# Down projection of a hybrid decoder layer: each pass opens with a plain pair of k tiles, the last pass takes its seventh sevenfold pair earlier, and GpSimd's additions go to VectorE

## The chip, the cores and the metric

One core of a Trainium2 chip runs the whole layer as one program. The metric is device time in microseconds (us), from the first to the last instruction and what lies around them, as the median of the runs shown. The engines are TensorE (PE; its weight loads are PEld), VectorE (DVE), ScalarE (ACT), GpSimd (POOL) and SyncE (SP), each with a queue of its own that is worked through in order. DMA transfers are issued from a queue (SP's for the weights, ScalarE's for the rest) and run beside the engines.

## What is computed

A decoder layer over 256 tokens of width 2048. Two token mixers and their merge come first; this change is in the last stage, the second matrix of the MLP:

```python
h = rmsnorm(x, norm_mlp_pre[l])
u = jnp.square(jax.nn.relu(h @ w_mlp_up[l]))          # 256 x 8192
x = x + rmsnorm(u @ w_mlp_down[l], norm_mlp_post[l])   # 8192 x 2048
```

All values are float32 and the result must agree with float32 arithmetic.

## The kernel before, in words

**Two parts for one number.** TensorE multiplies float32r here, which keeps fewer bits than float32. So every operand is split in two parts, hi (a rounded copy, ScalarE, L94) and lo (what is left, VectorE, L95), and a product is three matmuls: hi by hi, hi by lo, lo by hi (`product`, L1036). Weights arrive raw by DMA and are split on the fly by the class `Stream`: four raw half chunks (`wraw`, 512 KB each), six `whi` and six `wlo`. A chunk is one pair of k tiles by 1024 columns, in two halves.

**The MLP in two halves.** The hidden width 8192 is taken in two halves f = 0, 1 of 4096. For each, the up projection makes the 16 pairs of k tiles of u (`a_pair`, whose last step L261 adds two PSUM banks and so frees them; `evacuate` squares and splits). Then `down` runs twice, n = 0 and 1, over 1024 columns of the result each: four passes, here called (f, n). The passes with f = 0 leave their sum in DRAM (`acc_away`); those with f = 1 add it, and the last pass, (1, 1), also normalises and stores.

**A pass.** A pass goes over 16 pairs p of k tiles. A plain pair is 2 halves x 4 banks x 3 matmuls = 24 products of 128x512. The pairs in `SEVEN` = 0, 2, ..., 12 are done by a fast 2x2 scheme with seven products instead of eight: 7 x 3 = 21 matmuls, for which u and the weights are first combined by additions. Those of the weights are `split_sums`: VectorE makes the sums T1, T3, T4 in a tile t (L123 to L126), ScalarE rounds it to thi (L129), VectorE makes tlo (L130). These three tiles come from the pool `big` of twelve 1 MB buffers, which it shares with the activations `uT`, the accumulators and the gain. A pass has eight PSUM banks: four named s (for the products P1, P6, Q5, N7; the up projection's pairs live in the same four) and four of their own, Q3, P2, Q4 and Cs. The four quarters of the result, (token half tb, column half i), end in Q4, Cs, P2 and Q3 (`PLACE`).

**The order of a pass.** The pairs come as 0, 1, 2, ..., 15. After the seventh sevenfold pair, 12, the four s banks are combined into four tiles `ready` (L1077 to L1081), and `early` adds the accumulator to them (L1145): on VectorE, but in the last pass for tb = 1 on GpSimd. Pairs 14 and 15 are held back (`held` = 2) and done quarter by quarter, so that `finish` (L1162) can take one bank while TensorE fills the next. In the last pass the quarters come as (0, 0), (0, 1), (1, 0), (1, 1), and after each second one `finish` does the norm (L334 to L336), the residual (L1175) and the store. `between` multiplies a quarter of the accumulator by the gain g3 (L1155) behind pairs 3, 5, 7 and 9 of the last pass; g3 is loaded by ScalarE's queue (L1184), and so is x1, the residual (L1149, called from `early`).

**What sets the order of the queues.** A scheduler orders the instructions of each engine by the order in which the program gives them, with some look-ahead, and puts in the waits. `Stream.ahead` runs the splits six halves ahead of TensorE. So the order in which the weights are listed (`chunks`, and `sums`, which says which of them are sevenfold) sets what VectorE, ScalarE and the weight loads do, and when.

Of the kernel before, what the change touches and what calls it, by code (L numbers as in the profile page):

```python
# [22 lines left out]
ALU = mybir.AluOpType  # L23
# [15 lines left out]
SEVEN = (0, 2, 4, 6, 8, 10, 12)  # L39
PAIRS = 16  # L40


# [124 lines left out]
def layer(tc, x, g_pre, pos_t, pos_row, inv_freq, vecs, sinks, gains, w_kv, w_q, w_xy, w_rg, w_g, w_rp, w_ap, w_out,  # L167
# [37 lines left out]
    for f in range(2):  # L205
        chunks += [w_up[32 * f + i] for i in range(32)]
        for n in range(2):
            sums.update(len(chunks) + i for i in SEVEN)
            chunks += [w_dn[(2 * f + n) * PAIRS + i] for i in range(PAIRS)]

# [832 lines left out]

    def down(f, n, uT, held, order, finish, early, between=lambda p: None):

# [7 lines left out]
        def step(p, parts, names):  # L1053
            for name in names:
                at, n2 = name
                b = PLACE[name]
                for i, (hi, lo) in enumerate(parts):
                    t = slice(at * P, at * P + P)
                    c = quarter(n2)
                    a = uT[p][:, i]  # L1060
                    product(banks[b], (a[:, 0, t], a[:, 1, t]), (hi[:, c], lo[:, c]), b in begun,
                            p == PAIRS - 1 and i == 1)
                    begun.add(b)

        ready = {}
        for p in range(PAIRS - held):
            if p in SEVEN:
                parts = ws.seven()
                for name, (i, w) in LEFT.items():
                    product(banks[name], (uT[p][:, 0, i], uT[p][:, 1, i]), parts[w], name in begun,  # L1070
                            p == SEVEN[-1] and name in ("P1", "P6", "Q5", "N7"))
                    begun.add(name)
                if p == SEVEN[-1]:
                    for name in ((1, 0), (0, 0), (1, 1), (0, 1)):
# [6 lines left out]
                    v.tensor_tensor(ready[0, 1], ready[1, 1], banks["N7"], ALU.add)  # L1081
                    early(ready)
            else:
                for i in range(2):
                    hi, lo = ws.half()
                    for name in order:
                        at, n2 = name
# [4 lines left out]
                        begun.add(b)  # L1092
            between(p)
        parts = [[ws.half(False) for i in range(2)] for p in range(held)]
        for name in order:
            for i in range(held):
                step(PAIRS - held + i, parts[i], (name,))
            finish(name, banks[PLACE[name]], ready[name])
        ws.ahead(ws.at - 1)

    for f in range(2):
# [3 lines left out]
        for p in range(PAIRS):  # L1105
# [11 lines left out]
            if f == 1 or p >= R2_AT:  # L1117
# [7 lines left out]
                full.clear()  # L1125
        order = [(1, 1), (1, 0), (0, 0), (0, 1)]
        if f == 0:
            for n in range(2):
# [5 lines left out]

                down(f, n, uT, 2, order, finish, lambda ready: None)
            continue
# [5 lines left out]
        def early(ready):  # L1142
            for (tb, i), t in ready.items():
                c = quarter(2 * n + i)
                (nc.gpsimd if n and tb else nc.vector).tensor_tensor(t, t, acc[tb][:, c], ALU.add)  # L1145
            if n == 1:
# [3 lines left out]

        def between(p):
            if p in (3, 5, 7, 9):
                tb, q = divmod((p - 3) // 2, 2)
                c = quarter(q)
                nc.vector.tensor_tensor(acc[tb][:, c], acc[tb][:, c], g3[:, c], ALU.mult)  # L1155
# [22 lines left out]
        n = 0  # L1178
        down(f, n, uT, 2, order, finish, early)
        n = 1  # L1180
# [3 lines left out]
        nc.scalar.dma_start(g3, gains[3].partition_broadcast(P))  # L1184
        down(f, n, uT, 2, [(0, 0), (0, 1), (1, 0), (1, 1)], finish, early, between)
    ctx2.close()
# [73 lines left out]
```

## Time and profile before

| what | value |
|---|---|
| median of 3 runs | 1527.35 us (1525.62 to 1528.20) |
| the profiled execution, its own time | 1523.52 us |
| its span, first to last instruction | 1521.7 us |
| granted clock of TensorE, mean | 0.999 |
| TensorE busy | 1506.0 us (99%) |
| VectorE busy | 1105.1 us (73%) |
| ScalarE busy | 831.3 us (55%) |
| GpSimd busy | 5.5 us, 11 instructions |
| first product of the first down pass | at 1003.36 us |
| last product of the kernel | starts at 1511.89 us |

The page lists the busy time of each engine over the whole span. The views of the trace give single instructions: when each began, how long it took, and in brackets how long its engine had sat idle before it and what ended that.

### The profile page before, as it was taken

How to read it: one execution, taken by the hardware profiler on the slowest of the kernel's cores; microseconds unless marked ns; L12 is line 12 of the kernel's file. 1: busy time of each engine (PE TensorE's matmuls, PEld its weight loads, DVE VectorE, ACT ScalarE, POOL GpSimd, SP SyncE). 2: the span in 40 equal slices, each digit the busy share in tenths (PEclk: the TensorE clock that was granted, in tenths of full speed). 3: DMA queues.
4: the chain of work that ended last, by engine and by line, in shares of the span. 5: the costliest groups of instructions: out<-in, count | busy, mean ns of one | idle time of the engine just before them, and what ended most of it. 6: DMA issues, size and time to landing. Idle time of an engine off the chain costs nothing.

```text
span 1521.7 us, 20058 instructions
## 1 busy us (share of the span) xinstructions
PE 1506.0 (99%) x7600; PEld 1263.7 (83%) x7600; DVE 1105.1 (73%) x1377; ACT 831.3 (55%) x1143; POOL 5.5 (0%) x11
## 2 busy tenths in 40 slices
PE   9999999999999999999999999999999999999997
PEld 7877778788888888888888888888888888888886
DVE  6666666857759867555667866688886766788897
ACT  6545645746556757444355655555444555555553
POOL 0000000000000000000000000000000000000001
PEclk9999999999999999999999999999999999999999
DMA  6645445354655565555764755556667655566665
GB/s 252 221 153 166 138 142 168 128 188 161 215 184 189 169 219 177 197 195 191 263 225 131 274 198 189 187 182 216 213 202 237 205 187 192 188 230 200 216 221 178
DMA packets 82896, 296.20 MB, mean 195 GB/s; under 512 B 9712, under 2 KB 9968, under 8 KB 81648
## 3 DMA queue, kind: packets, MB, share of 16 engines
q1 hardware_dynamic: 79056, 284.43, 56.4%
q10 hardware_dynamic: 3744, 10.50, 1.9%
q8 instruction: 59, 0.97, 0.3%
q14 instruction: 37, 0.30, 0.1%
HBM read 288.60 MB, written 6.29 MB: 194 GB/s over the span
## 4 chain that ended last, share of the span: by engine, by line
PE 90%; DVE 4%; ACT 2%; DMA 2%; issue 2%; SPq 0%; DVEq 0%; ACTq 0%
PE ps L253 21%; PE ps L256 11%; PE dQ L1036 8%; PE s L1036 4%; PE pp L273 4%; PE pp L275 4%; PE pp L271 4%; PE dP L1036 4%; PE g L271 4%; PE g L275 4%; PE g L273 4%; PE dCs L1036 3%; PE q L271 2%; PE q L273 2%; PE q L275 2%
## 5 line engine op out<-in xcount | busy, mean ns | idle before, releaser
L95 DVE TENSOR_TENSOR wlo<-wraw,whi 128x1024 fp32r<-128x1024 f32 x523 | 634.4, 1222 | 306.2 <-ACT whi L94 304.6
L94 ACT CAST whi<-wraw 128x1024 fp32r<-128x1024 f32 x523 | 544.3, 1051 | 567.4 <-PE ps L253 139.2
L253 PE MATMUL ps<-h2T,whi 128*128 128x512 f32 x960 | 240.5, 393 | 0.0
L253 PEld LDWEIGHTS ps<-h2T,whi 128*128 128x128 f32 x960 | 172.9, 189 | 30.7
L256 PEld LDWEIGHTS ps<-h2T,wlo 128*128 128x128 f32 x960 | 131.0, 191 | 9.3
L256 PE MATMUL ps<-h2T,wlo 128*128 128x256 f32 x960 | 133.9, 283 | 0.0
L253 PE MATMUL ps<-hT,whi 128*128 128x512 f32 x512 | 130.0, 394 | 0.0
L1036 PE MATMUL dQ<-whi,uT 128*128 128x512 f32 x288 | 107.0, 389 | 0.0
L253 PEld LDWEIGHTS ps<-hT,whi 128*128 128x128 f32 x512 | 91.8, 189 | 16.8 <-issue 0.7
L271 PE MATMUL g<-whi,hT 128*128 128x512 f32 x256 | 101.7, 397 | 0.0
L273 PE MATMUL g<-wlo,hT 128*128 128x512 f32 x256 | 100.4, 392 | 0.1
L275 PE MATMUL g<-whi,hT 128*128 128x512 f32 x256 | 100.2, 391 | 0.0
L256 PEld LDWEIGHTS ps<-hT,wlo 128*128 128x128 f32 x512 | 69.8, 191 | 6.3 <-issue 1.5
L256 PE MATMUL ps<-hT,wlo 128*128 128x256 f32 x512 | 71.9, 283 | 0.0
L1036 PEld LDWEIGHTS dQ<-whi,uT 128*128 128x128 f32 x288 | 54.1, 188 | 11.2
L271 PEld LDWEIGHTS g<-whi,hT 128*128 128x128 f32 x256 | 48.1, 188 | 10.9 <-issue 1.3
L275 PEld LDWEIGHTS g<-whi,hT 128*128 128x128 f32 x256 | 48.1, 188 | 10.6 <-issue 0.7
L273 PEld LDWEIGHTS g<-wlo,hT 128*128 128x128 f32 x256 | 48.2, 188 | 9.7 <-DVE wlo L95 0.5
L1036 PE MATMUL dQ<-wlo,uT 128*128 128x512 f32 x144 | 56.1, 389 | 0.0
L130 DVE TENSOR_TENSOR tlo<-t,thi 128x1536 fp32r<-128x1536 f32 x28 | 49.2, 1757 | 6.8 <-ACT thi L129 6.8
L1036 PE MATMUL dP<-whi,uT 128*128 128x512 f32 x144 | 54.1, 389 | 0.0
L1036 PE MATMUL dCs<-whi,uT 128*128 128x512 f32 x144 | 54.1, 389 | 0.0
(280 smaller groups left out, 2477.4 us busy)
## 6 DMA issues: line engine op xcount, KB each, us to landing
wraw<-in_w_up SPq DMA_DIRECT2D x128, 512.0 KB, 4.7
wraw<-in_w_dn SPq DMA_DIRECT2D x128, 512.0 KB, 4.6
wraw<-in_w_g SPq DMA_DIRECT2D x64, 512.0 KB, 4.8
wraw<-in_w_xy SPq DMA_DIRECT2D x64, 512.0 KB, 4.6
wraw<-in_w_q SPq DMA_DIRECT2D x32, 512.0 KB, 3.7
wraw<-in_w_ap SPq DMA_DIRECT2D x32, 512.0 KB, 4.7
wraw<-in_w_rp SPq DMA_DIRECT2D x32, 512.0 KB, 4.4
wraw<-in_w_out SPq DMA_DIRECT2D x32, 512.0 KB, 5.2
```

Of the source, the lines that this page charges most:

```text
L94: self.pin(self.nc.scalar.copy(hi, src))
L95: self.pin(self.nc.vector.tensor_tensor(lo, src, hi.bitcast(F32), ALU.subtract))
L130: v.tensor_tensor(lo, t, hi.bitcast(F32), ALU.subtract)
L253: mm(both, hi[:, k * P : k * P + P], a.rearrange("p a b -> p (a b)"), start=half == 0 and k == 0, stop=False)
L256: mm(ps[:, f, 1, :], lo[:, k * P : k * P + P], a[:, 0, :], start=False, stop=half == 1 and k == 7)
L271: mm(banks[tb][n], a[:, 0, t], hi[:, n * 512 : n * 512 + 512], start=first, stop=False)
L273: mm(banks[tb][n], a[:, 0, t], lo[:, n * 512 : n * 512 + 512], start=False, stop=False)
L275: mm(banks[tb][n], a[:, 1, t], hi[:, n * 512 : n * 512 + 512], start=False, stop=last)
L1036: mm(b, a[x], w[y], start=not begun and i == 0, stop=tail and i == 2)
```

## The change

The order of the pairs within a pass is now a table: `PASS` for the first three passes and `LAST_PASS` for the last. A pass opens with the plain pair 1, and this first plain pair is done bank by bank (`step`: both halves into Q3, then P2, Q4, Cs) instead of half by half. Then come pair 0, 3, 2, 5, 4 and so on; pair 12 follows directly on pair 10. In the last pass pair 6 follows directly on pair 4, and pair 12 stands ahead of pair 11 instead of behind it. The list of weights follows the same tables, so loads and splits move with them. Plain pairs take the banks in the order `DOWN_ORDER` in every pass. `between` now counts places instead of pairs, and all additions of `early` are on VectorE.

```diff
+PASS = (1, 0, 3, 2, 5, 4, 7, 6, 9, 8, 11, 10, 12, 13, 14, 15)
+LAST_PASS = (1, 0, 3, 2, 5, 4, 6, 7, 8, 9, 10, 12, 11, 13, 14, 15)
...
         for n in range(2):
-            sums.update(len(chunks) + i for i in SEVEN)
-            chunks += [w_dn[(2 * f + n) * PAIRS + i] for i in range(PAIRS)]
+            turns = LAST_PASS if (f, n) == (1, 1) else PASS
+            sums.update(len(chunks) + i for i, p in enumerate(turns) if p in SEVEN)
+            chunks += [w_dn[(2 * f + n) * PAIRS + p] for p in turns]
...
-    def down(f, n, uT, held, order, finish, early, between=lambda p: None):
+    DOWN_ORDER = ((1, 1), (1, 0), (0, 0), (0, 1))
+
+    def down(turns, uT, held, order, finish, early, between=lambda i: None):
...
-                            p == PAIRS - 1 and i == 1)
+                            p == turns[-1] and i == 1)
...
-        for p in range(PAIRS - held):
+        final = [p for p in turns if p in SEVEN][-1]
+        for at_turn, p in enumerate(turns[:PAIRS - held]):
             if p in SEVEN:
...
-                if p == SEVEN[-1]:
+                if p == final:
...
+            elif not at_turn:
+
+                step(p, [ws.half() for i in range(2)], DOWN_ORDER)
             else:
                 for i in range(2):
                     hi, lo = ws.half()
-                    for name in order:
+                    for name in DOWN_ORDER:
...
-            between(p)
+            between(at_turn)
...
-                step(PAIRS - held + i, parts[i], (name,))
+                step(turns[PAIRS - held + i], parts[i], (name,))
...
-                (nc.gpsimd if n and tb else nc.vector).tensor_tensor(t, t, acc[tb][:, c], ALU.add)
+                nc.vector.tensor_tensor(t, t, acc[tb][:, c], ALU.add)
...
-        def between(p):
-            if p in (3, 5, 7, 9):
-                tb, q = divmod((p - 3) // 2, 2)
+        def between(i):
+            if i in (2, 4, 7, 9):
+                tb, q = divmod((2, 4, 7, 9).index(i), 2)
```

The rows of the order that follow name tiles with their numbers; `whi358` is the hi part of half chunk 358. The first pass begins with half 336, so half 336 + 2k belongs to the k-th pair of its order; the last pass begins with half 496.

TensorE's queue at the opening of the first pass, before (`s` is a bank that the up projection used, `dQ` and `dP` are banks of the pass, `seven` is u of a sevenfold pair):

```order
L1036 MATMUL s_8647<-whi_8509,seven_7318 128x512
L1036 MATMUL s_8647<-wlo_8510,seven_7318 128x512
L1036 MATMUL s_8647<-whi_8509,seven_7318 128x512
L1036 MATMUL dQ_8650<-whi_8509,seven_7318 128x512
L1036 MATMUL dQ_8650<-wlo_8510,seven_7318 128x512
L1036 MATMUL dQ_8650<-whi_8509,seven_7318 128x512
```

The same place now (`uT` is u of plain pairs):

```order
L1040 MATMUL dQ_8638<-whi_8503,uT_7069 128x512
L1040 MATMUL dQ_8638<-wlo_8504,uT_7069 128x512
L1040 MATMUL dQ_8638<-whi_8503,uT_7069 128x512
L1040 MATMUL dQ_8638<-whi_8533,uT_7069 128x512
L1040 MATMUL dQ_8638<-wlo_8534,uT_7069 128x512
L1040 MATMUL dQ_8638<-whi_8533,uT_7069 128x512
L1040 MATMUL dP_8637<-whi_8503,uT_7069 128x512
```

The sevenfold pair 0, with its s banks, has moved behind the 24 products of pair 1.

ScalarE's queue in the first pass around the cast `thi360` of pair 12, before (half 360 + 2 = 362 is pair 13 there):

```order
L129 CAST thi356_8932<-t356_8931 128x1536
L94 CAST whi360_9014<-wraw360_8947 128x1024
L94 CAST whi361_9018<-wraw361_8961 128x1024
L94 CAST whi362_9061<-wraw362_8992 128x1024
L94 CAST whi363_9065<-wraw363_8994 128x1024
L129 CAST thi360_9009<-t360_9008 128x1536
```

The same place now, where half 358 is pair 10, half 360 pair 12 and half 364 the first of the held pair 14:

```order
L132 CAST thi358_8968<-t358_8967 128x1536
L97 CAST whi361_9030<-wraw361_8953 128x1024
L97 CAST whi362_9052<-wraw362_8983 128x1024
L97 CAST whi363_9070<-wraw363_8997 128x1024
L97 CAST whi364_9097<-wraw364_9036 128x1024
L132 CAST thi360_9021<-t360_9020 128x1536
```

The cast of pair 12 comes one sevenfold pair behind that of pair 10 with no plain pair between them, and the cast of half 364 is ahead of it.

VectorE's queue at the opening of the last pass, before (L1162 finishes a bank of the pass ahead, `wlo498` is the first split of that pass's pair 1):

```order
L1162 TENSOR_TENSOR acc0_11505<-dQ4_11513,t_11993 128x512
L123 TENSOR_TENSOR t500_12125<-wraw501_12123,wraw500_12045 128x1024
L95 TENSOR_TENSOR wlo498_12116<-wraw498_12013,whi498_12115 128x1024
L1162 TENSOR_TENSOR acc0_11505<-dCs_11514,t_11995 128x512
L95 TENSOR_TENSOR wlo499_12120<-wraw499_12015,whi499_12119 128x1024
```

The same place now (`wlo498` belongs to pair 0, the second of the pass):

```order
L1172 TENSOR_TENSOR acc0_11493<-dQ4_11501,t_11993 128x512
L1172 TENSOR_TENSOR acc0_11493<-dCs_11502,t_11995 128x512
L1165 TENSOR_TENSOR acc0_11493<-acc0_11493,g3_12136 128x512
L98 TENSOR_TENSOR wlo498_12114<-wraw498_12013,whi498_12113 128x1024
L98 TENSOR_TENSOR wlo499_12118<-wraw499_12015,whi499_12117 128x1024
L98 TENSOR_TENSOR wlo500_12124<-wraw500_12033,whi500_12123 128x1024
L98 TENSOR_TENSOR wlo501_12145<-wraw501_12127,whi501_12144 128x1024
```

The first multiplication by g3 has moved from the middle of the pass to ahead of its second pair's splits, and the load of g3 on ScalarE's queue from behind the cast of half 503 to ahead of that of half 498.

## Rows read from the trace of the kernel before

**Rows 1.** The page: busy time, share of the span and instructions of each engine.

```profile
PE 1506.0 (99%) x7600; PEld 1263.7 (83%) x7600; DVE 1105.1 (73%) x1377; ACT 831.3 (55%) x1143; POOL 5.5 (0%) x11
```

**Rows 2.** Waits of TensorE, 840 to 1520 us: waiter, releaser: us in total, times, longest.

```profile
PE s L1036 <- DVE u L261: 0.5, 1, 0.5
```

**Rows 3.** Timeline, TensorE, first pass: start, duration, instruction [idle before, releaser].

```profile
1003.36 0.40 PE L1036 MATMUL s<-whi,seven 128*128 128x512 f32 x1
...
1006.56 0.39 PE L1036 MATMUL dQ<-thi,seven 128*128 128x512 f32 x1
1007.50 0.50 PE L1036 MATMUL s<-thi,seven 128*128 128x512 f32 x1 [0.55 <-DVE u L261]
1007.83 0.40 PE L1036 MATMUL s<-tlo,seven 128*128 128x512 f32 x1
```

**Rows 4.** Timeline, TensorE, last pass: first products of pairs 10, 11 and 12.

```profile
1480.84 0.39 PE L1036 MATMUL s<-whi,seven 128*128 128x512 f32 x1
...
1485.60 0.39 PE L1036 MATMUL dQ<-whi,uT 128*128 128x512 f32 x1
...
1491.04 0.39 PE L1036 MATMUL s<-whi,seven 128*128 128x512 f32 x1
```

**Rows 5.** Chain that ended last, in the first pass's opening: start, us, what.

```profile
1005.62 1.23 DVE wlo L95
1006.84 0.61 DVE u L261
```

**Rows 6.** Timeline, VectorE and ScalarE, last pass: splits of pair 10, then others.

```profile
1471.95 1.22 DVE L123 TENSOR_TENSOR t<-wraw,wraw 128x1024 f32<-128x1024 f32 x1
...
1474.05 1.05 ACT L94 CAST whi<-wraw 128x1024 fp32r<-128x1024 f32 x1 [3.44 <-DVE wraw L125]
...
1475.66 1.49 ACT L129 CAST thi<-t 128x1536 fp32r<-128x1536 f32 x1 [0.56 <-DVE t L126]
...
1477.18 1.76 DVE L130 TENSOR_TENSOR tlo<-t,thi 128x1536 fp32r<-128x1536 f32 x1 [0.42 <-ACT thi L129]
...
1478.85 2.36 DVE L95 TENSOR_TENSOR wlo<-wraw,whi 128x1024 fp32r<-128x1024 f32 x2
```

**Rows 7.** Timeline, all engines: additions at the end of pass (1, 0), then the tail.

```profile
1418.23 1.89 DVE L1145 TENSOR_TENSOR t<-t,acc 128x512 f32<-128x512 f32 x3
...
1500.73 1.22 DVE L95 TENSOR_TENSOR wlo<-wraw,whi 128x1024 fp32r<-128x1024 f32 x1
...
1503.73 0.39 PE L1036 MATMUL dQ<-whi,uT 128*128 128x512 f32 x1
1503.79 2.38 DVE L1145 TENSOR_TENSOR t<-t,acc 128x512 f32<-128x512 f32 x2
...
1503.95 1.67 POOL L1145 TENSOR_TENSOR t<-t,acc 128x512 f32<-128x512 f32 x1 [0.85 <-DVE t L1081]
...
1506.09 0.68 DVE L1162 TENSOR_TENSOR acc<-dQ,t 128x512 f32<-128x512 f32 x1
...
1506.80 0.63 ACT L1166 ACTIVATE spare<-acc 128x512 f32<-128x512 f32 x1 [6.41 <-DVE acc L1162]
...
1507.41 0.69 DVE L1162 TENSOR_TENSOR acc<-dCs,t 128x512 f32<-128x512 f32 x1
...
1511.89 0.39 PE L1036 MATMUL dQ<-whi,uT 128*128 128x512 f32 x1
...
1512.87 0.68 DVE L1162 TENSOR_TENSOR acc<-dQ,t 128x512 f32<-128x512 f32 x1
```

**Rows 8.** DMA issues of the whole run: transfer, queue, count, KB each, median us to landing.

```profile
wraw<-in_w_dn SPq DMA_DIRECT2D x128, 512.0 KB, 4.6
...
wraw<-in_w_q SPq DMA_DIRECT2D x32, 512.0 KB, 3.7
...
x<-x_away ACTq DMA_DIRECT2D x2, 1024.0 KB, 7.2
...
g<-in_gains ACTq DMA_DIRECT2D x1, 1024.0 KB, 8.7
```

More of the change, by code (lines that the diff above doesn't have):

```diff
@@ L1070, in down @@
                     product(banks[name], (uT[p][:, 0, i], uT[p][:, 1, i]), parts[w], name in begun,
-                            p == SEVEN[-1] and name in ("P1", "P6", "Q5", "N7"))
+                            p == final and name in ("P1", "P6", "Q5", "N7"))
                     begun.add(name)
-                if p == SEVEN[-1]:
+                if p == final:
                     for name in ((1, 0), (0, 0), (1, 1), (0, 1)):
@@ L1125, in layer @@
                 full.clear()
-        order = [(1, 1), (1, 0), (0, 0), (0, 1)]
+        order = DOWN_ORDER
         if f == 0:
@@ L1133, in finish @@
                     nc.scalar.dma_start(acc_away[tb][:, c], t)
-                down(f, n, uT, 2, order, finish, lambda ready: None)
+                down(PASS, uT, 2, order, finish, lambda ready: None)
             continue
@@ L1178, in layer @@
         n = 0
-        down(f, n, uT, 2, order, finish, early)
+        down(PASS, uT, 2, order, finish, early)
         n = 1
@@ L1184, in layer @@
         nc.scalar.dma_start(g3, gains[3].partition_broadcast(P))
-        down(f, n, uT, 2, [(0, 0), (0, 1), (1, 0), (1, 1)], finish, early, between)
+        down(LAST_PASS, uT, 2, [(0, 0), (0, 1), (1, 0), (1, 1)], finish, early, between)
     ctx2.close()
```

## The prediction

> **What bounds the kernel now.** I read the page's engine shares first, then what TensorE waited for, then the timeline of the places that the change touches. TensorE is busy 1506.0 of 1521.7 us [rows 1]: a change of order can win only where TensorE waits, or behind its last product. From 840 us to the end, the four down passes among it, the view of waits lists one wait of TensorE alone, 0.5 us on the addition L261 [rows 2]. The timeline shows it in the opening of the first down pass: products start at 1006.56, then at 1007.50, then at 1007.83 [rows 3]. The undisturbed pace comes from the last pass: a sevenfold pair of 21 products takes 1480.84 to 1485.60, a plain pair of 24 takes 1485.60 to 1491.04 [rows 4], 0.227 us a product. So the stall cost (0.94 - 0.23) + (0.33 - 0.23) = **0.8 us**. The chain says why: the addition L261, which frees the banks of the last up pair, ran behind a split L95 on VectorE and ended at 1007.45 [rows 5].
>
> The end is different. TensorE's last product ends at 1511.89 + 0.39 = 1512.28, and VectorE takes that bank only at 1512.87 [rows 7], being busy until then with the other half of the tokens. The rest is a chain of VectorE, ScalarE and the store: 1521.7 - 1512.28 = 9.4 us behind the last product.
>
> VectorE is the engine with little room. Its work for a sevenfold pair runs from 1471.95 to 1478.85, 6.9 us (some 6.5 without the wait on ScalarE's cast); for a plain pair it takes 2.36 [rows 6]. That is 9.3 of the 10.2 us that TensorE takes for the two.
>
> **The change, part by part.** The products are the same in number and kind; only places move.
>
> *The opening.* Each pass now opens with pair 1, bank by bank, on four banks that no up pair uses. The late banks are wanted at the sixteenth product of the sevenfold pair, which starts 24 x 0.227 = 5.4 us later than now: 5.4 + 3.4 = 8.8 us into the pass. L261 ended 1007.45 - 1003.36 = 4.1 us into it [rows 3, 5], so it is in time. **Gain 0.8 us**, once: the other three openings show no wait, so nothing is won there. In exchange the bank Cs, the last that the pass before gives up, is wanted after 18 products, 4.1 us, instead of 30. VectorE has its addition (0.69 us, as in the first row L1162 [rows 7]) and a split or two ahead of that: about 3 us. I cost it at nothing; if that cover goes, TensorE waits for what VectorE is behind.
>
> *Two sevenfold pairs in a row, first pass.* Every pass now has pair 10 directly ahead of pair 12. In the first pass only three buffers are free for t, thi and tlo, so thi and tlo of pair 12 lie where tlo and thi of pair 10 lay, and ScalarE's cast waits for pair 10's last products. I count from the last product but one of pair 8's sevenfold step: with pairs 11 and 10 behind it, the buffer is free after 45 products and a drain, 10.2 + 0.4 = 10.6 us. Cast 1.49 and VectorE 1.76 [rows 6]: tlo is there at 13.9, and TensorE wants it 61 products on, at 13.8. But the cast of half 364 stands ahead on ScalarE, and its load goes out only when VectorE has read the first half of pair 12, behind thi 1.49, tlo 1.76 and two additions of 1.22 and 0.69: at 5.6. It lands 4.6 us later [rows 8], its cast takes 1.05 [rows 6]: 11.2, so tlo is done at 14.5. Bounds: 0.1 us lost if the load is early, 3.3 if it takes the 7.2 us of x1's loads [rows 8]. I take **0.6 us lost**, by the median landing. The later passes have more free buffers, and there the cast of pair 12 waits for older pairs: nothing.
>
> *The last pass.* Here pairs 4 and 6 follow each other too. Two sevenfold pairs cost VectorE 13 us while TensorE takes 9.5, so 3.5 us are drawn from VectorE's lead. The lead now: tlo of pair 10 ends at 1478.94 and is wanted 13 products behind 1480.84 [rows 4, 6], 4.8 us later. That suffices if VectorE starts the pass in time. And here the order moves what the diff does not name: the multiplication of the accumulator by the gain g3 (L1155, now L1165) stands ahead of the splits 498 and 499 on VectorE, and ScalarE issues the load of g3 ahead of the pass. I put that 2.6 us ahead of the opening: bank P2's last product 5.3 us ahead, its addition 0.7, the cast of pair 0 in between 1.5, a square and its read 0.8 [rows 6, 7]. If g3 lands L us after issue, split 498 ends at L - 2.6 + 0.6 + 1.2 into the pass; TensorE wants it after 25 products, 5.7, and waits when L exceeds 6.5. Later it is tighter: from there VectorE has 3 splits, 3 multiplications, the sevenfold pairs 2, 4 and 6 and plain pair 5, 3.5 + 1.8 + 19.5 + 2.4 = 27.2 us, and some 1.5 us of waits for loads, until tlo of pair 6, which TensorE wants 148 products in, at 33.5. With L = 5.0 that is 4.2 + 28.7 = 32.9, 0.6 in hand; it decides from about **L = 5.7 us**. Rows for L: 3.7 us for 512 KB at the quickest, 7.2 for x1's 1 MB, 8.7 for g3 as it is now, beside weights [rows 8]. When it is issued now, the weight buffers are all full or held and hardly a load goes beside it, so I take 5.0, nearer to the first, and cost this at **0.1 us**; ends 0 and 3.0 (8.7 - 5.7).
> By the Trainium skill, "DMA: Bandwidth & Descriptors", section "Anatomy of one DMA", a transfer takes 2.0 us and its bytes at 436 GB/s, fitted on the GpSimd path: an estimate of 4.4 us for 1 MB, by which nothing is lost. No row here shows a load of 1 MB alone.
>
> *The tail without GpSimd.* Now VectorE's two additions L1145 beside GpSimd's take 2.38 us, where three without it took 1.89 [rows 7]: 1.1 us more than they need, and VectorE reaches bank Q4 at 1506.09 although its last product ended at 1503.73 + 0.39. All four additions now come some 5 us earlier, since pair 12 does. VectorE then meets the banks at TensorE's pace: Cs ends 24 products ahead of the last, at 1506.84, instead of being taken at 1507.41, and the last bank is taken at about 1512.35 instead of 1512.87. **Gain 0.5 us**; more is not to be had, as TensorE ends there, and if VectorE is late again it is 0.
> By the Trainium skill, "SBUF — State Buffer", section "SBUF: two separate sides", an operation of VectorE with two SBUF inputs and one of GpSimd that reads SBUF shut each other out for a whole instruction; by that the additions would lose up to GpSimd's 1.67 us, where the row shows 1.1.
> The loads of x1 now go out behind, not ahead of, most of the last weight loads. Split 527 ended at 1501.95 and was wanted 37 products ahead of the last one, at 1503.5 [rows 7]: 1.5 us in hand. I count nothing, with 1 us lost as the other end.
>
> **Sum**: -0.8 - 0.5 + 0.6 + 0.1 = -0.6 us against the profiled execution's 1523.52. The median of the runs shown is 3.8 us above that; I keep that difference: 1527.35 - 0.6 = **1526.8 us**.
>
> **The rivals.**
> *All seams are covered*, chance 0.20: half 364 lands early and g3 in time, -1.3 us, 1526.1. For it: TensorE waited once in 680 us. Against it: the count gives tlo of pair 12 no slack even at best.
> *g3 holds up the last pass*, 0.20, the one that ends slower: its load takes the 8.7 us of now, VectorE stands in front of split 498, TensorE loses 3.0, the sum is +2.3 and the time 1529.7. TensorE waits from L = 5.7 us, and the whole is slower from 6.4. For it: every row of a 1 MB load is over 7. Against it: each of those had company.
> *The change doesn't do what it says*, 0.05: the opening's wait comes back on bank Cs and the tail stays VectorE's: no difference, 1527.4.
> *The forecast* has 0.55.
>
> **How the numbers follow.** 0.2%, about what a measurement of this kernel can tell from no change, is 3.05 us. No case reaches it by itself. Faster by that much takes more than twice all the gains there are; only scatter as in the runs shown, 1525.62 to 1528.20, could show it: 0.04. Slower takes g3's 3.0 together with an upper end at a seam or at the tail: 0.08. The rest is 0.88. The range goes from the covered case less half the scatter, 1524.6, to the g3 case and a little more, 1530.0.
>
> **What would show it.** Right: no wait of TensorE on the up pair's addition in the first pass; the last bank taken within 0.1 us of TensorE's last product; 8.9 us instead of 9.4 behind that product; a gap of some tenths ahead of the first product with tlo of pair 12 in the first pass. Wrong: a wait of TensorE on a split some 5.7 us into the last pass, with VectorE idle on g3 ahead of it; a gap at another pair of sevenfold neighbours; a wait for the splits 524 to 527; or a gain over 1.5 us, for which I know no place.

## The result and the profile after

The changed kernel took 1533.43 us, median of 9 runs (1529.14 to 1536.23). The kernel before, beside it, took 1526.76 us (9 runs, 1525.62 to 1528.20). The ratio is 1.004, with an interval of 1.0029 to 1.0051: 6.7 us slower by the medians, where 0.6 us faster was forecast. The profiled execution of the changed kernel took 1529.14 us, its span is 1527.4: it is the quickest of its runs, so it shows the least of the loss. (The profiled execution of before, 1523.52 us, lies 3.2 us below its median, that of the changed kernel 4.3: the two profiles compare quick executions.)

The page, engine shares (answers to [rows 1]):

```profile
PE 1508.9 (99%) x7600; PEld 1262.8 (83%) x7600; DVE 1106.1 (72%) x1379; ACT 830.3 (54%) x1143; POOL 1.7 (0%) x9
```

The work is the same; TensorE only stands longer. Its view of waits from 840 us to the end (answers to [rows 2]; waiter, releaser: us in total, times, longest):

```profile
PE dP L1040 <- DVE wlo L98: 1.4, 2, 0.8
PE dQ L1040 <- DVE wlo L98: 1.0, 2, 0.8
PE dQ L1040 <- DVE tlo L133: 0.5, 2, 0.3
PE dQ L1040 <- ACT whi L97: 0.4, 1, 0.4
PE dP L1040 <- ACT whi L97: 0.3, 1, 0.3
```

The wait on the up pair's addition is gone, and five kinds of waits on splits of weights have come. The timeline puts all of them in the last pass. TensorE, last pass, the eight products that waited: the first two belong to pair 6, the next three to pair 12, the last three to the held pairs 14 and 15.

```profile
1462.95 0.50 PE L1040 MATMUL dP<-wlo,seven 128*128 128x512 f32 x1 [0.60 <-DVE wlo L98]
1464.86 0.49 PE L1040 MATMUL dQ<-tlo,seven 128*128 128x512 f32 x1 [0.25 <-DVE tlo L133]
...
1489.08 0.49 PE L1040 MATMUL dP<-whi,seven 128*128 128x512 f32 x1 [0.34 <-ACT whi L97]
1490.34 0.50 PE L1040 MATMUL dP<-wlo,seven 128*128 128x512 f32 x1 [0.77 <-DVE wlo L98]
1492.25 0.50 PE L1040 MATMUL dQ<-tlo,seven 128*128 128x512 f32 x1 [0.26 <-DVE tlo L133]
...
1507.03 0.50 PE L1040 MATMUL dQ<-whi,uT 128*128 128x512 f32 x1 [0.40 <-ACT whi L97]
1508.29 0.50 PE L1040 MATMUL dQ<-wlo,uT 128*128 128x512 f32 x1 [0.76 <-DVE wlo L98]
1509.51 0.50 PE L1040 MATMUL dQ<-wlo,uT 128*128 128x512 f32 x1 [0.27 <-DVE wlo L98]
```

Counted against the pace of 0.227 us a product, with the slower product behind each wait, and taken from the starts of the products, that is 1.5 us at pair 6, 2.2 at pair 12 and 2.3 at the held pairs: 6.0 in all. Two theories come out of the rows around them.

*Neighbours.* VectorE's timeline in the last pass, pairs 4 and 6 (the first row of each is its first sum, L133 its last part):

```profile
1450.19 1.22 DVE L126 TENSOR_TENSOR t<-wraw,wraw 128x1024 f32<-128x1024 f32 x1 [0.36 <-issue]
...
1454.41 1.23 DVE L98 TENSOR_TENSOR wlo<-wraw,whi 128x1024 fp32r<-128x1024 f32 x1 [0.52 <-ACT whi L97]
1455.79 1.76 DVE L133 TENSOR_TENSOR tlo<-t,thi 128x1536 fp32r<-128x1536 f32 x1 [0.15 <-ACT thi L132]
1457.46 1.22 DVE L126 TENSOR_TENSOR t<-wraw,wraw 128x1024 f32<-128x1024 f32 x1
...
1463.04 1.76 DVE L133 TENSOR_TENSOR tlo<-t,thi 128x1536 fp32r<-128x1536 f32 x1 [0.15 <-ACT thi L132]
```

From the first sum of one to the first sum of the other are 7.27 us: with no plain pair's splits to put in between, VectorE stands 0.52 and 0.15 us on ScalarE's casts within each. Two of them take 14.5 us while TensorE takes 9.5.

*Loads of x1.* They go out together at 1493.94 us, where before they had gone out at 1484.68 and 1487.89. Issues in the stretch 1492 to 1507 (count, KB each, median us to landing):

```profile
wraw<-in_w_dn SPq DMA_DIRECT2D x4, 512.0 KB, 9.6
x<-x_away ACTq DMA_DIRECT2D x2, 1024.0 KB, 9.5
```

Over the whole run of before such a load took 4.6 us [rows 8]. But those near the end had x1's loads beside them there too; in the kernel before, stretch 1485 to 1500:

```profile
wraw<-in_w_dn SPq DMA_DIRECT2D x4, 512.0 KB, 7.7
```

So the last weights take 9.6 us instead of 7.7. The chain that ended last shows one of these loads ahead of the held pairs' last wait: 1496.77 to 1507.05 is a load, then ScalarE's cast, then the split, then the product at 1509.51.

### The profile page after: what moved, and what is told of

It reads as the page before. It is cut to its first block, busy times and chain, and to the rows that moved or that the text cites. A ratio compares the mean times of both kernels' runs of the same rounds, so it can differ in the third digit from the quotient of the medians.

```text
span 1527.4 us, 20056 instructions
## 1 busy us (share of the span) xinstructions
PE 1508.9 (99%) x7600; PEld 1262.8 (83%) x7600; DVE 1106.1 (72%) x1379; ACT 830.3 (54%) x1143; POOL 1.7 (0%) x9
## 4 chain that ended last, share of the span: by engine, by line
PE 89%; DVE 5%; DMA 3%; ACT 2%; issue 1%; DVEq 0%; SPq 0%; ACTq 0%
PE ps L257 22%; PE ps L260 11%; PE dQ L1040 6%; PE pp L275 4%; PE pp L277 4%; PE pp L279 4%; PE g L275 4%; PE s L1040 4%; PE g L279 4%; PE g L277 4%; PE dP L1040 3%; PE dCs L1040 2%; DMA wraw<-in_w_dn 2%; PE q L275 2%; PE q L277 2%; PE q L279 2%
## 5 line engine op out<-in xcount | busy, mean ns | idle before, releaser
L133 DVE TENSOR_TENSOR tlo<-t,thi 128x1536 fp32r<-128x1536 f32 x28 | 49.2, 1758 | 6.2 <-ACT thi L132 5.9
```

What stands on the lines that cost most here:

```text
L133: v.tensor_tensor(lo, t, hi.bitcast(F32), ALU.subtract)
```

## The experiments

All sixteen kernels and both originals in one table. The stages are read from the timeline of TensorE in each profiled execution: from the first product of pass (0, 0) to the first of the second up projection; from the first product of pass (1, 0) to the start of the last; from there to the end of the span. The up projection between took 178.74 or 178.75 us in every one. The ratio is against the kernel before, run beside it. "New" is `PASS`, "old" is 0, 1, ..., 15, "free" is 1, 0, 3, 2, ..., 13, 12, 14, 15: opened with pair 1, no sevenfold neighbours. "Own" is `LAST_PASS`.

The stages of a row come from one execution, the ratio from all of them. What lies ahead of the first pass is the same work in every kernel, yet the first product of that pass started anywhere from 1003.03 to 1004.99 us: differences of a microsecond or two between two spans can come from there.

| run | passes (0,0), (0,1) / (1,0) / (1,1) | first two | last two | behind | median us | ratio (interval) |
|---|---|---|---|---|---|---|
| before | old | 165.43 | 164.36 | 9.81 | 1526.76 | 1 |
| changed | new / new / its own | 165.30 | 170.35 | 9.37 | 1533.43 | 1.0040 (1.0029-1.0051) |
| last_old | new / new / old | 167.67 | 165.42 | 11.21 | 1529.35 | 1.0017 (1.0006-1.0028) |
| x1_last | as changed, x1 late | 168.12 | 169.31 | 9.29 | 1530.95 | 1.0028 (1.0016-1.0039) |
| last_as_pass | new / new / new | 168.27 | 170.37 | 9.31 | 1532.17 | 1.0033 (1.0020-1.0045) |
| no_neighbours | new / new / free | 167.84 | 171.04 | 10.31 | 1531.73 | 1.0034 (1.0021-1.0047) |
| old_openings | new / new / own, two open with 0 | 166.04 | 172.20 | 9.39 | 1530.70 | 1.0023 (1.0013-1.0032) |
| none_near | free / free / free, x1 late | 164.59 | 166.72 | 10.36 | 1527.72 | 1.0001 (0.9991-1.0010) |
| first_only | (0,0) new, the rest old | 165.91 | 164.40 | 11.21 | 1527.58 | 1.0002 (0.9993-1.0012) |
| vector_adds | old, no GpSimd | 165.37 | 165.40 | 11.15 | 1527.15 | 0.9995 (0.9986-1.0004) |
| near_first | old, 12 behind 10 in three passes | 166.82 | 173.62 | 11.18 | 1536.76 | 1.0068 (1.0055-1.0080) |
| mix | free / free / old, x1 late | 164.93 | 168.58 | 10.05 | 1527.92 | 1.0010 (1.0001-1.0018) |
| x1_before | old, x1 late | 165.52 | 165.13 | 9.54 | 1524.85 | 0.9988 (0.9979-0.9997) |
| last_near | free / free / its own, x1 late | 164.59 | 170.74 | 9.35 | 1529.99 | 1.0022 (1.0013-1.0031) |
| best | free / old / old, x1 late | 164.59 | 164.98 | 10.35 | 1524.14 | 0.9980 (0.9970-0.9990) |
| best_near | free / old / 12 behind 10, x1 late | 164.59 | 166.99 | 9.40 | 1525.08 | 0.9985 (0.9976-0.9994) |
| last_ns | free / old / free, x1 late | 164.58 | 164.84 | 11.02 | 1525.31 | 0.9989 (0.9981-0.9998) |
| no_gain | as last_ns, without g3 | 164.58 | 164.79 | 11.34 | 1524.94 | 0.9982 (0.9973-0.9991) |

### Where the loss lies: last_old, x1_last, last_as_pass, no_neighbours

**last_old**, against the changed kernel:

```diff
-LAST_PASS = (1, 0, 3, 2, 5, 4, 6, 7, 8, 9, 10, 12, 11, 13, 14, 15)
+LAST_PASS = (0, 1, 2, 3, 4, 5, 6, 7, 8, 9, 10, 11, 12, 13, 14, 15)
...
-            if i in (2, 4, 7, 9):
+            if i in (3, 5, 7, 9):
```

> The last pass goes back to the pairs in the order 0, 1, ..., 15; the first three passes and the additions on VectorE stay as changed. Theory 1 (the whole loss lies in the last pass, where pairs 4 and 6, and 10 and 12, are neighbours, and where x1 is loaded late): no wait of TensorE in the last pass, the opening of the first pass stays repaired (0.8 us won), its seam at pair 12 costs 0.2 to 0.3, so 0.3 to 0.8 us below the kernel before: 1526 us. Rival (the new order costs in the three other passes too): still 2 us or more above the kernel before, with waits in passes 1 to 3.

Over half of the loss goes, but 1529.35 is still 2 us above. The first two passes took 167.67 us here, and 167.8 to 168.3 in the three runs below, although their order is that of the changed kernel, whose one profiled execution has 165.30. So the rival holds too: pass (0, 1) loses 2.8 to 3.4 us in four of the five profiled executions with that order, and 0.45 in the one of the changed kernel.

**x1_last**: `early` no longer loads x1; a function called when the held pairs' weights are split does, behind the last cast:

```diff
-            if n == 1:
-                for tb in range(TB):
+        def residual_in():
+            with tc.issue_after(ws.cast.ins):
+                for tb in range(TB):
                     x1.append(flat(unit(f"x1{tb}", F32)))
                     nc.scalar.dma_start(x1[tb], x1_away[tb])
```

> As changed, but the two loads of x1 are issued behind the cast of half 527, the last one. Theory 2 (x1's 2 x 1 MB beside the weights of the held pairs makes those weights late): the three waits at pairs 14 and 15, 0.57 + 1.14 + 0.55 = 2.25 us, are gone, the weight loads there land in 4 to 5 us instead of 10, the waits at pairs 6 and 12 stay: 2 to 2.5 us below the changed kernel, about 1531, and less scatter. Rival (VectorE is behind there for its own reasons): the waits stay, under 0.5 us won. A miss of another kind would be a wait of the residual on x1 in the tail, if the loads take more than 6 us now.

As theory 2 had it, no product of the held pairs waits any more. By the ratios 1.8 us are won (1.0040 to 1.0028), but the two intervals overlap, so this run alone does not show the gain; x1_before below does. The scatter is not much less, 1528.51 to 1534.03, and the last pass loses 0.9 us at pair 2, which the changed kernel did not. The issues in the stretch 1492 to 1507 are now

```profile
wraw<-in_w_dn SPq DMA_DIRECT2D x6, 512.0 KB, 4.9
```

instead of 9.6 us. By the Trainium skill, "DMA: Bandwidth & Descriptors", section "Queues, rings and completion order", each DMA engine takes turns between the queues that have work for it; 9.6 against 4.9 agrees. This run's TensorE also shows what pass (0, 1) loses (pair 2, then pair 12 twice, then a held pair):

```profile
1105.83 0.50 PE L1040 MATMUL dQ<-tlo,seven 128*128 128x512 f32 x1 [0.89 <-DVE tlo L133]
...
1150.88 0.50 PE L1040 MATMUL dP<-wlo,seven 128*128 128x512 f32 x1 [0.55 <-DVE wlo L98]
1152.79 0.50 PE L1040 MATMUL dQ<-tlo,seven 128*128 128x512 f32 x1 [0.25 <-DVE tlo L133]
1162.98 0.50 PE L1040 MATMUL dQ<-wlo,uT 128*128 128x512 f32 x1 [0.37 <-DVE wlo L98]
```

**last_as_pass** and **no_neighbours** change one line, to

```diff
+LAST_PASS = (1, 0, 3, 2, 5, 4, 7, 6, 9, 8, 11, 10, 12, 13, 14, 15)
...
+LAST_PASS = (1, 0, 3, 2, 5, 4, 7, 6, 9, 8, 11, 10, 13, 12, 14, 15)
```

> The last pass in the order of the three others: a plain pair between 4 and 6, pair 12 still behind pair 10. Theory 1 (two sevenfold pairs in a row take VectorE 14.5 us while TensorE takes 9.5): the waits at pair 6 (1.3 us) go, those at pair 12 stay or shrink little (up to 2.2 us), those at the held pairs stay: 1 to 2 us below the changed kernel. Rival (the load and the multiplications by g3 ahead of the splits make VectorE late from the opening on): TensorE still waits for a split in the first third of the pass, since these stand where they stood.

> The last pass in the order 1, 0, 3, 2, ..., 13, 12, 14, 15, without sevenfold neighbours. Theory 1: no wait of TensorE up to the held pairs, 3.6 us won against the changed kernel; what is left of the held pairs' 2.25 us belongs to the loads of x1 (theory 2). So 1527 to 1530 us. Rival (g3 ahead of the splits): the waits move but 2 us or more of them stay in the first two thirds of the pass.

Theory 1 holds in both: with a plain pair between 4 and 6 no wait of TensorE stands there any more (0.17 and 0.09 us of delay are left), with one between 10 and 12 too there is none up to the held pairs. The waits at pair 12 in last_as_pass are those of the changed kernel. But no time is won, because x1's loads come later still: 1.73 us of waiting at once in last_as_pass and 3.19 in no_neighbours, on ScalarE's cast of a late load (none_near below has the last pass of no_neighbours with x1's loads late, and no wait at the held pairs). From no_neighbours:

```profile
1509.14 0.80 PE L1040 MATMUL dQ<-whi,uT 128*128 128x512 f32 x1 [3.19 <-ACT whi L97]
1510.40 0.79 PE L1040 MATMUL dQ<-wlo,uT 128*128 128x512 f32 x1 [0.46 <-DVE wlo L98]
```

### Neighbours or the new opening: old_openings, none_near, near_first

In pass (0, 1) VectorE stands still where the pass opens, since the loads of the next sevenfold pair go out late. VectorE in x1_last; in the changed kernel the same wait is 2.56 us:

```profile
1097.48 1.22 DVE L126 TENSOR_TENSOR t<-wraw,wraw 128x1024 f32<-128x1024 f32 x1 [4.72 <-DMA wraw<-in_w_dn]
```

That made the opening a suspect. **old_openings** (against the changed kernel; passes (0, 1) and (1, 1)) and **none_near** (with x1 late):

```diff
+SECOND_PASS = (0, 1, 3, 2, 5, 4, 7, 6, 9, 8, 11, 10, 12, 13, 14, 15)
+LAST_PASS = (0, 1, 3, 2, 5, 4, 6, 7, 8, 9, 10, 12, 11, 13, 14, 15)
...
+PASS = (1, 0, 3, 2, 5, 4, 7, 6, 9, 8, 11, 10, 13, 12, 14, 15)
+LAST_PASS = PASS
```

> The changed kernel, but passes (0, 1) and (1, 1), which follow straight on another pass, open with the sevenfold pair 0 again instead of with pair 1 (order 0, 1, 3, 2, ...). The neighbours 10 and 12, and 4 and 6 in the last pass, stay. Theory A (opening with a plain pair there costs VectorE its lead: at that seam the weight buffers hold pairs 0 and 3, the loads of pair 2 go out only when pair 0 is split, and VectorE stands 2.5 to 4.7 us without weights): VectorE's wait for a load at these two seams shrinks by 2 us or more; TensorE's 1 to 3.5 us of waits in pass (0, 1) go to under 0.5, those at pairs 6 and 12 of the last pass to under half of their 3.6 us; about 1528 to 1530 with x1 still late. Rival B (the neighbours alone overload VectorE): the waits at pair 12 of both passes and at pair 6 stay as they are.

> The other half: all four passes open with pair 1 and run 1, 0, 3, 2, ..., 13, 12, 14, 15, so no two sevenfold pairs are neighbours anywhere; x1's loads behind the last cast. Theory A: TensorE still waits 1 to 3 us in pass (0, 1) and VectorE still stands at both seams between passes, though in the last pass the lead may last to the held pairs. Rival B: no wait of TensorE in any pass but for some tenths, about 1526.

Neither theory stands whole. With the old openings pass (0, 1) loses 0.85 us instead of some 3, and VectorE's wait for a load there shrinks to 0.86, as theory A had it. But the waits at pairs 6 and 12 of the last pass stay, and two others join them, at pairs 1 and 2. The first of these is the prediction's g3 rival: here g3's load took 8.0 us, beside weight loads, and the split that TensorE wants stands behind the multiplication that waits for it (1.45 us lost):

```profile
1434.53 0.69 DVE L1166 TENSOR_TENSOR acc<-acc,g 128x512 f32<-128x512 f32 x1 [3.14 <-DMA g<-in_gains]
...
1436.41 0.50 PE L1041 MATMUL dQ<-wlo,uT 128*128 128x512 f32 x1 [1.15 <-DVE wlo L99]
```

With the new openings but no neighbours TensorE does not wait once in the first two passes: 164.59 us, 0.84 less than before, just what the opening's stall had cost. VectorE still stands 4.07 us at the seam there; it has that much in hand. So the opening alone costs nothing in pass (0, 1), and the 3 us of that pass were seen only where the new opening and the neighbours came together. Rival B misses as well: TensorE waits 1.72 us in the last pass, at pair 4, and the median is that of the kernel before, not 1526.

**near_first** has the neighbours without the opening, in the kernel before:

```diff
+PASS = (0, 1, 2, 3, 4, 5, 6, 7, 8, 9, 11, 10, 12, 13, 14, 15)
```

> The kernel before, opening and all, but in the first three passes pairs 10 and 11 change places, so that 12 follows directly on 10. Theory N (sevenfold neighbours near a pass's end draw on VectorE's lead, and the lead is short from there into the next pass): the two first passes, with 165.4 us in the kernel before, take 166.5 to 168, with waits of TensorE at pair 12 and the held pairs of pass (0, 1); 1529. Rival (opening with a plain pair is what costs): no wait but the opening's, 165.4 us, as the kernel before.

The kernel is 10 us slower, so neighbours cost without the new opening. But they do not cost where theory N put it: pass (0, 1) has no wait, and takes the 82.44 us of before. The loss lies at pair 12 of the first pass (2.2 us) and in one stall of 4.33 us at a held pair of pass (1, 0), where the same pass in last_old, with 10 and 12 as neighbours and the same old pass behind it, had none. VectorE there:

```profile
1422.03 1.23 DVE L126 TENSOR_TENSOR t<-wraw,wraw 128x1024 f32<-128x1024 f32 x1 [2.96 <-DMA wraw<-in_w_dn]
1423.17 0.69 DVE L1086 TENSOR_TENSOR t<-s,t 128x512 f32<-128x512 f32 x1
...
1425.57 1.89 DVE L1155 TENSOR_TENSOR t<-t,acc 128x512 f32<-128x512 f32 x3
1427.37 1.22 DVE L98 TENSOR_TENSOR wlo<-wraw,whi 128x1024 fp32r<-128x1024 f32 x1
```

The split that TensorE wants is queued behind the first sums of the next pass's pair 0, whose load is late, and behind seven additions.

### The small terms: first_only, vector_adds

**first_only** is the kernel before with `PASS` in pass (0, 0) alone, **vector_adds** the kernel before with one line changed:

```diff
-                (nc.gpsimd if n and tb else nc.vector).tensor_tensor(t, t, acc[tb][:, c], ALU.add)
+                nc.vector.tensor_tensor(t, t, acc[tb][:, c], ALU.add)
```

> The kernel before, with the new order in pass (0, 0) alone; the three other passes and GpSimd's additions as before. Theory A: the opening's 0.8 us are won, 0.2 lost at pair 12, no other wait of TensorE: 0.6 us below the kernel before, about 1526.4, and scatter like that of the kernel before. Rival (the new order costs in the first pass too, or in what follows it): at or above the kernel before, with waits of TensorE behind the first pass.

> The kernel before, with the four additions of the last pass all on VectorE; the order stays. By the tail of the run with the old last pass (11.2 us behind TensorE's last product, against 9.4): about 1.8 us slower, 1528.8, since VectorE reaches the first finished bank 1.8 us later and with it the chain behind. Rival (GpSimd's additions slow VectorE's, as the prediction had it: 1.1 us of VectorE's time are given back): slower by 0.7 us or less.

Neither can be told from the kernel before. first_only wins the 0.8 and loses 0.3 at pair 12 and 1.0 in pass (0, 1), 0.8 of it at pair 4: its rival was right that the new order also costs in the pass behind it. vector_adds shows neither 1.8 us nor 0.7; its interval ends 0.6 us above the kernel before. The 11.15 us behind its last product are not the additions': first_only, with GpSimd, has 11.21. There the last casts come 1.3 us later against the last product than in the profiled execution of before, and they waited for their loads, which went beside x1's. That these loads are the cause is not shown: mix and best, with x1 late and the old last pass, have 10.05 and 10.35.

### Late x1, and which pass bears a new order: mix, x1_before, last_near

All three load x1 as x1_last does; **x1_before** is the kernel before with that alone.

```diff
+PASS = (1, 0, 3, 2, 5, 4, 7, 6, 9, 8, 11, 10, 13, 12, 14, 15)
+LAST_PASS = (0, 1, 2, 3, 4, 5, 6, 7, 8, 9, 10, 11, 12, 13, 14, 15)
...
+LAST_PASS = (1, 0, 3, 2, 5, 4, 6, 7, 8, 9, 10, 12, 11, 13, 14, 15)
```

(mix, and the second line that last_near has in its place.)

> The first three passes open with pair 1 and have no sevenfold neighbours (1, 0, 3, 2, ..., 13, 12, 14, 15), the last pass in the old order, x1's loads behind the last cast, GpSimd's additions as before. Theory N and theory 2 (x1's loads late): no wait of TensorE in the first two passes (164.6 us), none in the last two (164.4), 9.4 to 9.8 us behind the last product: 1.5 to 3 us below the kernel before, 1525. Rival (what the last pass of the changed kernel lost comes from the opening of the pass ahead): 2 us of waits in the last pass, 1527.5 or more.

> The kernel before with x1's loads behind the last cast, nothing else. Theory 2: the last weight loads land in 5 us or less whatever the run, what lies behind TensorE's last product is 9.4 to 9.8 us in every run instead of up to 11.2, so 1 to 1.5 us below the kernel before. Rival: x1 is now late for the residual and VectorE waits for it in the tail: slower by 1 us or more.

> The first three passes without neighbours, x1's loads late, but the last pass in the order of the change, with 4 and 6, 10 and 12 as neighbours. Theory N1 (the last pass's neighbours alone cost what was seen): waits at pair 6 and pair 12 of 3.5 us or more, 169 us for the last two passes, 1530 to 1531. Rival N2 (the lead was drawn by the neighbours 10 and 12 at the end of the pass ahead): under 2 us of waits in the last pass, 1528.

x1_before is 1.6 us faster than the kernel before by the medians (0.9979 to 0.9997): loading x1 late pays in the old order too. (That 9.4 to 9.8 us lie behind the last product in every run is not borne out; see best and mix.) last_near shows the waits at pairs 6 and 12 with no neighbours in the passes ahead, so N2 falls. But it also lost 0.9 us at pair 3 and 2.05 at pair 4, where its one wait is the 1.72 us of none_near; VectorE was behind before it came to the neighbours, so what they cost on a full lead is not shown here. mix misses: 2.31 us of waiting in its last pass, though that has the old order. Both point to pass (1, 0), whose "free" order puts pair 12, and with it VectorE's eight additions behind it (four that combine the s banks, four of the accumulator), right ahead of the held pairs.

### The last questions: best, best_near, last_ns, no_gain

Three tables, x1 late, GpSimd's additions as before:

```diff
+PASS = (1, 0, 3, 2, 5, 4, 7, 6, 9, 8, 11, 10, 13, 12, 14, 15)
+THIRD_PASS = (0, 1, 2, 3, 4, 5, 6, 7, 8, 9, 10, 11, 12, 13, 14, 15)
+LAST_PASS = (0, 1, 2, 3, 4, 5, 6, 7, 8, 9, 10, 11, 12, 13, 14, 15)
...
+LAST_PASS = (0, 1, 2, 3, 4, 5, 6, 7, 8, 9, 10, 12, 11, 13, 14, 15)
...
+LAST_PASS = (1, 0, 3, 2, 5, 4, 7, 6, 9, 8, 11, 10, 13, 12, 14, 15)
```

(best; then the last line of best_near; then that of last_ns and no_gain.)

> The two passes with f = 0 open with pair 1 and have no sevenfold neighbours (1, 0, 3, 2, ..., 13, 12, 14, 15); the two with f = 1 keep the old order; x1's loads behind the last cast; GpSimd's additions as before. If the loss lies where a pass with f = 1 is reordered (neighbours, or the late start of the last pass): 164.6 us for the first two passes, 165 for the last two, 9.5 behind the last product, 0.8 us below the kernel before with late x1 alone, about 1524. Rival (an opening with pair 1 costs in the pass behind it too): waits in pass (0, 1) or no gain over that kernel.

> As the run best, but in the last pass pairs 11 and 12 change places, so that 12 follows on 10: the change's seventh sevenfold pair two places ahead, alone. Theory N1 (neighbours cost wherever they stand): 1.5 to 2.2 us of waits at pair 12 and up to 1 us behind it. Rival (they only cost where the lead has been drawn on before): under 0.5 us of waits, and the same time as the run best or a little less, since VectorE has the additions earlier.

> As the run best, but the last pass in the order 1, 0, 3, 2, ..., 13, 12, 14, 15. There is no neighbour anywhere, and pass (1, 0) ends as in the kernel before. Theory S (the seam: opening the last pass with pair 1 makes VectorE start late there, whatever stands behind): 1.5 to 2.5 us of waits in the first half of the last pass. Rival (the lead was lost by the order of pass (1, 0)): no wait, the same time as the run best.

> As the run last_ns, but the gain g3 is left out: neither its load nor the multiplications by it (the last ones are copies). Theory G (g3's load beside the first weights of the last pass and its multiplications on VectorE are what makes it late): the waits of the run last_ns go. Theory S: they stay, or shrink by the 1.8 to 2.4 us of multiplications at most.

**best beats both kernels**: 0.998 (0.997 to 0.999) of the kernel before, 2.9 us by the medians. Against x1_before (0.9979 to 0.9997) the gain of the reordering is not clear of the noise; in the stages it is the opening's 0.84 us. best_near: no wait at pair 12, where N1 expected 1.5 to 2.2 us, but two at the held pairs, 1.16 and 0.17 us; against best it loses 2.0 us ahead of the last product and gets 0.95 back behind it, where the additions come earlier. last_ns has the changed opening and no wait in its last pass, so theory S falls; no_gain is the same within the scatter, so g3 is not the cause either. What mix and none_near lost was lost by the order of pass (1, 0): mix and best differ in that alone, 168.58 and 164.98 us. The traces suggest how. The eight additions run from 9.3 to 3.2 us ahead of the last pass in mix, from 14.9 to 8.9 in best, and from 17.5 to 8.8 in last_old, where `PASS` stands in pass (1, 0). The first sum for pair 2 then begins 5.4 us into the last pass in mix, and 1.3 and 1.7 in the others. In mix the split of pair 3 that TensorE waits for, at 1448.59, stands behind the sums of pair 4, whose load is late:

```profile
1434.83 1.22 DVE L126 TENSOR_TENSOR t<-wraw,wraw 128x1024 f32<-128x1024 f32 x1
...
1446.72 1.23 DVE L126 TENSOR_TENSOR t<-wraw,wraw 128x1024 f32<-128x1024 f32 x1 [3.40 <-DMA wraw<-in_w_dn]
...
1448.59 1.22 DVE L98 TENSOR_TENSOR wlo<-wraw,whi 128x1024 fp32r<-128x1024 f32 x1
```

In best the first of these rows, the sum for pair 2, is

```profile
1430.99 1.23 DVE L127 TENSOR_TENSOR t<-wraw,wraw 128x1024 f32<-128x1024 f32 x1 [1.70 <-DMA wraw<-in_w_dn]
```

The rows thus put the cost on the additions at the seam between two passes; no run moves them alone, so this is argued and not shown.

## Why the prediction was wrong

**The opening: right.** Predicted 0.8 us won; the first two passes take 0.84 less wherever nothing else is lost. "Once" was read from one quick execution: x1_before, vector_adds and best_near, which open pass (1, 0) with pair 0, lose 0.6 to 0.8 us on the same addition there, and the new opening loses nothing. In x1_before:

```profile
1352.19 0.50 PE L1036 MATMUL s<-thi,seven 128*128 128x512 f32 x1 [0.47 <-DVE u L261]
```

In the changed kernel the sevenfold pair begins 5.47 us into the first pass, as counted (5.4), and no product of it waits:

```profile
1003.64 0.40 PE L1040 MATMUL dQ<-whi,uT 128*128 128x512 f32 x1
...
1009.11 0.39 PE L1040 MATMUL s<-whi,seven 128*128 128x512 f32 x1
```

**The first pass's seam: right in kind.** Predicted 0.6, measured 0.2, at the product with tlo of pair 12 as said (0.23 us ahead of it and behind it); the load of half 364 landed 3.65 us after its issue, where 4.6 was taken:

```profile
1068.17 0.50 PE L1040 MATMUL dQ<-tlo,seven 128*128 128x512 f32 x1
1068.50 0.39 PE L1040 MATMUL dQ<-thi,seven 128*128 128x512 f32 x1
```

**The step that failed first** is the sentence "The later passes have more free buffers, and there the cast of pair 12 waits for older pairs: nothing." It asked only for buffers. What neighbours use up is VectorE's lead, and the sentence has no term for that. The runs showed 2.2 us lost at pair 12 of the last pass (2.4 in last_as_pass), and, together with the new opening, some 3 us in pass (0, 1) in four profiled executions out of five. In pass (1, 0) "nothing" was right: no product waits there in any profiled execution with the changed kernel's `PASS`. The same sum stood two sentences further on for pairs 4 and 6, "13 us while TensorE takes 9.5", and was not made for 10 and 12. It was mis-sized as well: 14.5 instead of 13, since the 0.4 us of waits on the casts that were taken off come back, as 0.67, in each sevenfold pair without a plain one beside it; two such pairs 0.75 us dearer each turn "0.6 in hand" into a loss, 1.5 us at pair 6. The prediction had named the sign, "a gap at another pair of sevenfold neighbours".

**The second** is "I count nothing, with 1 us lost as the other end" for x1's loads. The held pairs lose 2.3 us in the profiled execution and nothing in x1_last. The 1.5 us in hand were right, but they had been read beside weight loads of 7.7 us; now, with both of x1's loads issued at once, these take 9.6. The rows of before held the warning: x1's own loads, and that of g3, took 7.2 and 8.7 us in company [rows 8]. This sign too, "a wait for the splits 524 to 527", had been named.

**The g3 rival** did not come true in the changed kernel. Issued at 1427.18 us, g3 landed 4.5 us later, predicted 5.0:

```profile
1427.18 0.34 ACTq L1194 DMA_DIRECT2D g<-in_gains  x1
...
1431.75 0.69 DVE L1165 TENSOR_TENSOR acc<-acc,g 128x512 f32<-128x512 f32 x1 [0.71 <-DMA g<-in_gains]
```

The Trainium skill's estimate of the prediction, 4.4 us by "DMA: Bandwidth & Descriptors", section "Anatomy of one DMA", agrees with that 4.5. TensorE did not wait at the pass's opening, and no_gain wins nothing measurable against last_ns. The rival's condition, a slow load, came true in old_openings: g3 took 8.0 us there, and TensorE lost 1.45 us on it. In last_ns it took 7.5, and TensorE did not wait.

**The tail: the size by luck, the cause half right.** Behind the last product's start the span lasts 9.37 instead of 9.81 us, 0.44 where 0.5 was predicted, and VectorE takes the last bank at once:

```profile
1518.03 0.39 PE L1040 MATMUL dQ<-whi,uT 128*128 128x512 f32 x1
1518.47 0.68 DVE L1172 TENSOR_TENSOR acc<-dQ,t 128x512 f32<-128x512 f32 x1
```

The prediction gave two reasons. The runs bear out pair 12's earlier place, and not leaving out GpSimd: best_near, with GpSimd, has 9.40, and vector_adds has no gain. An addition takes 0.68 us there, where beside GpSimd one of VectorE's two took 1.78 in the kernel before. But VectorE with four of them comes to the first bank as late as with two beside GpSimd: 4.46 us ahead of the last product's start, in vector_adds and in first_only. And 9.81 was a low value for the old order: both these runs have 11.2, so against them the tail won 1.8.

**The sum** for the profiled execution: -0.84 opening, -0.44 tail, +0.71 lost in the first two passes (0.3 of it the seam, 0.4 at the held pairs of pass (0, 1)), +6.0 in the last pass (3.7 at the neighbours, 2.3 at the held pairs), together +5.4; its span is 5.7 longer, and the other 0.3 lie ahead of the first pass (its first product comes at 1003.64 instead of 1003.36). The median adds what pass (0, 1) loses in most of the profiled executions. The forecast's terms kept their sign, but for g3's 0.1, which came to nothing; the two steps counted at nothing were the largest. The range ended at 1530.0 because it was drawn from the g3 case, and no case had either of them in it.

## What to carry to other kernels

An engine that only feeds the bound engine, and is nine tenths busy doing so, has a lead that is an account: ask of each reordering what it draws, where it is paid back, and what stands in line behind it, in every pass and not only where a buffer is short. Two heavy items in a row draw it at once, and the bill may come a pass later. A large load that moves towards the end is to be priced by the weights that it slows down, not by itself; issuing it behind the last of them won 0.12% here by itself (0.9988), where the whole reordering lost 0.4%.

## What the runs showed of the hardware

A stall of some length costs more than itself. In near_first TensorE had stood 4.33 us; windows of TensorE around it (busy us and count, granted clock, DMA share, GB/s):

```profile
1418.00:1424.00 6.00, 6.00 (x28) 1.00 0.62 244
1424.00:1428.00 4.00, 0.32 (x2) 0.99 0.00 0
1428.00:1431.00 3.00, 2.35 (x6) 0.50 0.39 130
1431.00:1434.00 3.00, 3.00 (x9) 0.50 0.77 253
1434.00:1437.00 3.00, 3.00 (x13) 0.87 0.40 147
```

The granted clock went to 0.50, 1.2 GHz, and only in the last of these windows back to full: products came 0.43 us apart instead of 0.23, and the 4.5 us lost at the stall became 7.4. The same followed 2.31 us of standing in mix (1.6 us more were lost at half clock) and 3.19 in no_neighbours. It did not follow the waits under 0.8 us of the changed kernel, nor 1.72 us in none_near and 1.73 in last_as_pass: their clock stays at 1.00. This is part of why no_neighbours, with fewer stalls, was no faster: its held pairs lost 6.6 us.
